# A hybrid encoder layer on one Trainium2 core: PSUM banks, gates, reciprocal roots and x blocks of the first pass

## The chip, the cores and the metric

The kernel runs on one core of a Trainium2 chip. Its engines are TensorE (PE), VectorE (DVE), ScalarE (ACT), GpSimd (POOL) and SyncE (SP, which here only issues DMAs); each runs its own list of instructions in order, and they wait for one another by semaphores. The metric is the device time of one execution in microseconds. Before the change it was 2523.88 us, the median of three runs (2520.88 to 2533.51).

## The reference

Two sequences of 2048 tokens (prompt and sample), 1024 features, go through one layer with the same weights.

```python
hx = rms_norm(x, pre_g)
proj = hx @ w_in                                   # 1024 -> 3088 columns
a_u, a_z, b_qkv, b_z, b_gates, c_qkv, c_z, d_q, d_z = split(proj)
y_a = fourier_mix(a_u, w_fnet) * silu(a_z)         # FFT over tokens and features
y_b = gdn_branch(b_qkv, b_gates, ...) * silu(b_z)  # 5-tap convolution, gated DeltaNet, both directions
y_c = neighbourhood_attn(c_q, c_k, c_v, rpb) * silu(c_z)
y_d = memory_attn(d_q, rms_norm(mem, mem_g), w_mem_kv) * silu(d_z)
out = x + rms_norm(concat(y_a, y_b, y_c, y_d) @ w_out, post_g)
```

Every `rms_norm` and `l2_norm` needs a reciprocal square root of a mean or a sum of squares.

## The kernel before, in words

Products are made in three matmuls of fp16 halves (high by high, high by low, low by high), so a weight is split once into `hi` and `lo` (`wnext`, L388 to L421) and x is split per block (`xblock`, L448).

The first pass (`pass_a`, L540) takes x in 16 blocks of 256 tokens, eight for each request (r = 0, 1). For a block, `xblock` loads two tiles of 128 tokens (`xt`), ScalarE sums the squares (L458), `rsqrt` (L232) makes the reciprocal root in eleven small VectorE operations (two on integers, then three rounds of three), ScalarE and VectorE write the halves `xh` (L466, L213), and two DMA transposes put them into `xT` (L468). From `xT` TensorE makes the units k, q, v (48 matmuls each, L484 to L486) and ag, which is 256 columns for the Fourier branch and 16 gate columns (2 times 24 matmuls, L494 to L496). Each unit has one of two PSUM banks with the tag `mm` in turn. ScalarE drains a bank to `st` (L561, L568) and stores it to DRAM (`braw`, `au`); the 16 gate columns are drained by VectorE (L569). A copy of `xT` goes to DRAM (`xTd`, L551) for the later passes.

The next stage, `gdn_pre` (L931), runs beside the first pass. For each of 16 tiles of 256 tokens `conv_pair` reads `braw` back with two tokens of either neighbour (`craw`, L885; two buffers) and convolves it: one ScalarE operation (L889) and four VectorE operations (L891) for each half of k, q and v. `norms` (L911) calls `rsqrt` on 16 columns for each tile. `gdn_gates` makes the decays. After that come the Fourier branch, the triangular solve (`gdn_sub`, VectorE and GpSimd), the memory attention, the recurrence over 32 steps (`gdn_chain`) with the neighbourhood attention beside it, and the output projection (`pass_o`). The second and third projections (`pass_b`, `pass_z`) fill TensorE beside them. `rsqrt` is called 18 times in `xblock` (two of them for the memory tokens), 16 times in `norms`, 8 times in `gdn_out` and 17 times in `pass_o`.

What stands where on an engine is not written by hand: the tile framework simulates the engines while it builds, and by its own costs and the priority of each `band` (L202) chooses the next instruction. So a change of one instruction can move many others. SP's DMAs run in the order in which they are listed, and a DMA that waits holds up those behind it.

At the start of the program SP also writes zeros around `braw` of both requests (L518, L519): columns of two floats, 768 rows each.

## Time and profile before

| | |
|---|---|
| median of three runs | 2523.88 us |
| profiled execution | 2518.5 us, its span 2516.7 us |
| PE, DVE busy | 2006.7 us (80%), 2013.1 us (80%) |
| ACT, POOL busy | 1034.4 us (41%), 1128.9 us (45%) |
| mean granted TensorE clock | 0.919 |

The profile is of one execution, and 1.8 us of its time lie outside its span. Stages are found by their tiles: the first convolution operation starts at 119.8 us, the first pass drains its last bank at 653.9 us, the last tile of `gdn_pre` ends its convolution at 857.9 us, the recurrence runs from 1472 to 2112 us, and the matmuls of the output projection from 2152 us. Busy shares are to be read stage by stage; the table of stretches further down gives them.

### The profile page before, as it was taken

What the parts mean: (1) busy time and instruction counts of PE and PEld (TensorE: products, weight loads), DVE (VectorE), ACT (ScalarE), POOL (GpSimd) and SP (SyncE); (2) the same over time, 40 slices, a digit from 0 to 9 for tenths busy, and PEclk for the clock granted to TensorE, in tenths of its full rate; (3) what the DMA queues carried; (4) which work ended last, traced back from release to release, by engine and by line L of the source; (5) the groups of instructions that cost most, each with busy time, mean ns of one, the idle gap of its engine ahead of it and who ended that gap; (6) DMA issues with size and microseconds to landing.
All of it is one profiled execution on the core that took longest, in us unless ns stands there. A gap on an engine that the chain in (4) does not pass through costs nothing. (4 is left out here: it accounts for less than half of the span.)

```text
span 2516.7 us, 60042 instructions
## 1 busy us (share of the span) xinstructions
PE 2006.7 (80%) x23715; PEld 1701.4 (68%) x23715; DVE 2013.1 (80%) x4757; ACT 1034.4 (41%) x2434; POOL 1128.9 (45%) x1181
## 2 busy tenths in 40 slices
PE   0787778787446786899698988887788899899998
PEld 0665667665335675777576767777677788688887
DVE  3579988989999979668989667887679977677774
ACT  1455554553354421334056423554445523332322
POOL 1225655445476667535786152232234343533220
PEclk9988899998768988999799999999999999899999
DMA  9899899999635694599789877999999995555543
GB/s 94 193 210 178 200 232 239 233 209 234 180 94 159 168 222 118 142 218 179 153 187 200 181 195 210 229 199 210 198 214 224 217 279 164 169 182 187 187 161 118
DMA packets 827484, 476.08 MB, mean 189 GB/s; under 512 B 556864, under 2 KB 789952, under 8 KB 818752
## 3 DMA queue, kind: packets, MB, share of 16 engines
q1 hardware_dynamic: 802624, 438.67, 76.0%
q10 hardware_dynamic: 24576, 33.56, 4.5%
q8 instruction: 186, 3.05, 0.5%
q14 instruction: 98, 0.80, 0.1%
HBM read 243.38 MB, written 163.73 MB: 162 GB/s over the span
## 5 line engine op out<-in xcount | busy, mean ns | idle before, releaser
L484 PE MATMUL pj<-xT,w 128*128 128x256 f16 x2592 | 741.1, 286 | 119.7 <-DMA xT<-xh 35.7
L486 PE MATMUL pj<-xT,w 128*128 128x256 f16 x2592 | 739.5, 285 | 4.0 <-POOL w L421 4.0
L485 PE MATMUL pj<-xT,w 128*128 128x256 f16 x2592 | 740.6, 286 | 0.0
L485 PEld LDWEIGHTS <-w 128*128 128x128 f16 x2592 | 265.1, 102 | 109.4 <-issue 67.7
L484 PEld LDWEIGHTS <-w 128*128 128x128 f16 x2592 | 265.1, 102 | 102.7 <-issue 31.4
L486 PEld LDWEIGHTS <-w 128*128 128x128 f16 x2592 | 265.3, 102 | 52.8 <-POOL w L421 9.4
L502 PE MATMUL po<-w,oy 128*128 128x256 f16 x1024 | 280.3, 274 | 1.4 <-DVE oy L716 1.4
L500 PE MATMUL po<-w,oy 128*128 128x256 f16 x1024 | 280.7, 274 | 0.8 <-ACT oy L715 0.8
L501 PE MATMUL po<-w,oy 128*128 128x256 f16 x1024 | 280.9, 274 | 0.0
L891 DVE SCALAR_TENSOR_TENSOR cacc<-craw,cws,cacc 128x256 f32<-128x256 f32 x384 | 244.4, 671 | 7.4 <-ACT cacc L889 6.2
L494 PE MATMUL pj<-w,xT 128*128 128x272 f16 (+1 forms) x512 | 153.3, 300 | 43.8 <-ACT st L561 21.8
L230 POOL TENSOR_TENSOR oy<-oy,oz 128x512 f32<-128x512 f32 x60 | 101.0, 1704 | 187.7 <-ACT oy L701 179.4
L1165 POOL COPY bk<-rA 64x512 f16<-64x512 f16 x124 | 85.8, 692 | 208.9 <-PE pw L502 171.2
L765 ACT ACTIVATE oj<-po,wsc_o 128x256 f32<-128x256 f32 x128 | 59.5, 469 | 243.9 <-PE po L502 243.1
L495 PE MATMUL pj<-w,xT 128*128 128x272 f16 (+1 forms) x512 | 153.0, 299 | 0.8 <-POOL w L421 0.8
L496 PE MATMUL pj<-w,xT 128*128 128x272 f16 (+1 forms) x512 | 152.9, 299 | 0.0
L421 POOL TENSOR_TENSOR w<-wt,w 128x512 f16<-128x512 f32 (+1 forms) x70 | 85.1, 1223 | 145.9 <-ACT w L419 118.4
L227 POOL TENSOR_TENSOR mP<-mP,mP 128x1024 f16<-128x1024 f32 x32 | 71.6, 2241 | 137.0 <-DVE ty L1503 52.9
L500 PE MATMUL pno<-nPT,nv 128*128 128x64 f16 x704 | 78.5, 199 | 57.9 <-DMA nPT<-np__2819_27983 20.2
L1170 DVE COPY b<-rA 64x1536 f16<-64x1536 f16 x128 | 112.4, 878 | 8.1 <-DMA cT<-T 3.7
L227 POOL TENSOR_TENSOR km<-kt,km 128x256 f16<-128x256 f32 x128 | 96.4, 775 | 38.0 <-ACT km L1009 36.2
L1485 ACT ACTIVATE mP<-pms,ty,mds 128x256 f32<-128x256 f32 x128 | 71.0, 560 | 97.7 <-DVE ty L1482 76.0
(442 smaller groups left out, 6162.7 us busy)
## 6 DMA issues: line engine op xcount, KB each, us to landing
xT<-xTd SPq DMA_DIRECT2D x32, 1024.0 KB
rec<-km SPq DMA_DIRECT2D x32, 768.0 KB
rA<-rec SPq DMA_DIRECT2D x64, 384.0 KB
xTd<-xT SPq DMA_DIRECT2D x16, 1024.0 KB
sz<-st ACTq DMA_DIRECT2D x64, 256.0 KB
oz<-sz SPq DMA_DIRECT2D x16, 1024.0 KB
out_dram<-oo SPq DMA_DIRECT2D x32, 512.0 KB
craw<-braw SPq DMA_DIRECT2D x48, 260.0 KB
```

Source lines behind the costliest of these rows:

```text
L227: self.nc.gpsimd.tensor_tensor(out=out, in0=a, in1=b, op=ALU.subtract)
L484: nc.tensor.matmul(ps, whi, xhi, start=(kt == 0), stop=False)
L485: nc.tensor.matmul(ps, whi, xlo, start=False, stop=False)
L486: nc.tensor.matmul(ps, wlo, xhi, start=False, stop=(kt == KT - 1))
L494: nc.tensor.matmul(ps, xhi, whi, start=(kt == 0), stop=False)
L495: nc.tensor.matmul(ps, xhi, wlo, start=False, stop=False)
L496: nc.tensor.matmul(ps, xlo, whi, start=False, stop=(kt == KT - 1))
L500: nc.tensor.matmul(ps, whi, xhi, start=start, stop=False)
L501: nc.tensor.matmul(ps, whi, xlo, start=False, stop=False)
L502: nc.tensor.matmul(ps, wlo, xhi, start=False, stop=stop)
L891: nc.vector.scalar_tensor_tensor(out=acc[:, f], in0=raw[:, f, t:t + CB], scalar=w[:, t:t + 1], in1=acc[:, f], op0=ALU.mult, op1=ALU.add)
L1170: nc.vector.tensor_copy(b1[s, :, h].rearrange("p (d x) c -> p d x c", d=2), ra[s, :, 0:12])
```

## The change

Five edits. `rsqrt` starts from one integer operation in place of two, and has one Newton round of three operations and one round of higher order of four: eight operations in place of eleven. The gate columns are drained by ScalarE in place of VectorE. In the first pass the units take four PSUM banks in turn: the two of `mm`, and those with the tags `s` and `t`, which attention and the Fourier branch use later. The first two x blocks of request 0 are transposed by TensorE (through the banks `s` and `t`, copied to `xT` by ScalarE) in place of the DMA. `craw` has four buffers, and the scheduler is told to list the load of `craw` behind the second unit after the next block's unit of the same name, and the first convolution operation behind the fourth (`behind`: an order for the scheduler, with no semaphore).

```diff
+    def behind(self, ins, i):
+        if i < len(self.gseq):
+            self.tc.add_manual_dep(ins.ins if hasattr(ins, "ins") else ins, self.gseq[i],
+                                   mybir.DependencyInfo(mybir.DependencyClass.NoSync, mybir.DependencyReason.DATA), reason="pace")
...
-        nc.vector.tensor_scalar(out=y.bitcast(I32), in0=x.bitcast(I32), scalar1=1, scalar2=None, op0=ALU.logical_shift_right)
-        nc.vector.tensor_scalar(out=y.bitcast(I32), in0=y.bitcast(I32), scalar1=-1.0, scalar2=float(0x5F3759DF),
-                                op0=ALU.mult, op1=ALU.add)
-        for i in range(3):
-            eng.scalar_tensor_tensor(out=t, in0=y, scalar=-0.5, in1=y, op0=ALU.mult, op1=ALU.mult)
-            eng.scalar_tensor_tensor(out=t, in0=t, scalar=1.0, in1=x, op0=ALU.mult, op1=ALU.mult)
-            eng.scalar_tensor_tensor(out=(out if i == 2 else y), in0=t, scalar=1.5, in1=y, op0=ALU.add, op1=ALU.mult)
+        stt = lambda o, a, s, b, op: eng.scalar_tensor_tensor(out=o, in0=a, scalar=s, in1=b, op0=op, op1=ALU.mult)
+        nc.vector.tensor_scalar(out=y.bitcast(I32), in0=x.bitcast(I32), scalar1=-0.5, scalar2=float(0x5F3759DF), op0=ALU.mult, op1=ALU.add)
+        stt(t, y, -0.5, y, ALU.mult)
+        stt(t, t, 1.0, x, ALU.mult)
+        stt(y, t, 1.5, y, ALU.add)
+
+        c = math.sqrt(0.375)
+        stt(t, y, c, y, ALU.mult)
+        stt(t, t, 1.0, x, ALU.mult)
+        stt(t, t, -1.25 / c, t, ALU.add)
+        stt(out, t, 1.875, y, ALU.add)
...
-            nc.sync.dma_start(dst[:, :, :, t * P:t * P + P].rearrange("p l k t -> p (l k) t"), hl.rearrange("p l c -> p (l c)"), transpose=True)
+            if pe:
+                for l in range(2):
+                    pt = self.pat.tile([P, KT, P], F16, name=self.nm("pxt"), tag=PSS[l])
+                    for k in range(KT):
+                        nc.tensor.transpose(pt[:, k], hl[:, l, k * P:k * P + P], self.ident16)
+                    nc.scalar.activation(dst[:, l, :, t * P:t * P + P], pt, AF.Copy)
+            else:
+                nc.sync.dma_start(dst[:, :, :, t * P:t * P + P].rearrange("p l k t -> p (l k) t"), hl.rearrange("p l c -> p (l c)"), transpose=True)
...
+    def bank(self, wide):
+        self.nbank += 1
+        if wide and self.nbank % 2:
+            return self.pat.tile([P, 2, 256], F32, name=self.nm("pj"), tag="st"[self.nbank // 2 % 2])
+        return self.pmm.tile([P, 2, 256], F32, name=self.nm("pj"), tag="mm")
...
-            xT = self.xblock(x[tb * 256:tb * 256 + 256, :])
+            xT = self.xblock(x[tb * 256:tb * 256 + 256, :], pe=r == 0 and tb < 2)
...
-                nc.vector.tensor_scalar(out=self.gates[r][:, 2 * tb + t, :], in0=ps[:, 256:272], scalar1=d, scalar2=None, op0=ALU.mult)
+                nc.scalar.activation(self.gates[r][:, 2 * tb + t, :], ps[:, 256:272], AF.Copy, scale=d)
...
-        raw = pp.tile([P, 2, CB + 4], F32, name=self.nm("craw"), tag="craw", bufs=2)
-        nc.sync.dma_start(raw, self.D[f"braw{r}"][:, 2 * i:2 * i + 2, tb * CB:tb * CB + CB + 4])
+        raw = pp.tile([P, 2, CB + 4], F32, name=self.nm("craw"), tag="craw", bufs=4)
+        g = self.gidx[r, min(tb + 1, 7), u]
+        self.behind(nc.sync.dma_start(raw, self.D[f"braw{r}"][:, 2 * i:2 * i + 2, tb * CB:tb * CB + CB + 4]), g + 2)
...
-            nc.scalar.activation(acc[:, f], raw[:, f, 0:CB], AF.Copy, scale=w[:, 0:1])
+            self.behind(nc.scalar.activation(acc[:, f], raw[:, f, 0:CB], AF.Copy, scale=w[:, 0:1]), g + 4)
```

Three places show how the order moves. The first is SP's list near its start (`w` with 128x8x64 rows are weights of v, `xt_654` and `xt_658` the two tiles of the second x block). Before:

```order
L456 DMA xt_654<-in_x_prompt_dram 128x1024
L518 DMA braw_3153<-ty_3154 768x1x2
L519 DMA braw_3153<-ty_3154 768x1x2
L468 DMA_TRANSPOSE xT_107<-xh_133 128x16x128
L468 DMA_TRANSPOSE xT_107<-xh_137 128x16x128
L385 DMA w_369<-in_w_in_dram 128x8x64
L385 DMA w_464<-in_w_in_dram 128x8x256
L385 DMA w_464<-in_w_in_dram 128x8x16
L551 DMA xTd_0_216<-xT_107 128x4096
L456 DMA xt_658<-in_x_prompt_dram 128x1024
```

And now, where `xt_689` and `xt_693` are those two tiles and `xt_1094` is the first of the third block:

```order
L469 DMA xt_689<-in_x_prompt_dram 128x1024
L548 DMA braw_3196<-ty_3197 768x1x2
L549 DMA braw_3196<-ty_3197 768x1x2
L469 DMA xt_693<-in_x_prompt_dram 128x1024
L469 DMA xt_1094<-in_x_prompt_dram 128x1024
L398 DMA w_404<-in_w_in_dram 128x8x64
L398 DMA w_499<-in_w_in_dram 128x8x256
L398 DMA w_499<-in_w_in_dram 128x8x16
L398 DMA w_2784<-in_w_in_dram 128x8x256
L581 DMA xTd_0_251<-xT_107 128x4096
```

The block's transposes are gone from the list, and the next x tiles have moved ahead of the weights of v and ag; the writes of zeros stay ahead of all of these.

The second is VectorE at the same time (`w_277` is q's raw weight, `w_369` v's; L415 scales, L431 takes the largest magnitude). Before:

```order
L409 TENSOR_SCALAR ty_279<-gpre,wsc_q 128x8
L333 TENSOR_REDUCE ty_628<-ty_623 32x1
L415 TENSOR_TENSOR wt_301<-w_277,ty_279 128x512
L415 TENSOR_TENSOR wt_305<-w_277,ty_279 128x512
L334 STREAM_TRANSPOSE pmb<-ty_628 32x32
L335 COPY ty_620<-pmb 32x1
L336 COPY ty_620<-pmb 32x1
L337 COPY ty_620<-ty_620 64x1
L431 TENSOR_REDUCE ty_377<-w_369 128x2 x4
L415 TENSOR_TENSOR wt_309<-w_277,ty_279 128x512
L415 TENSOR_TENSOR wt_313<-w_277,ty_279 128x512
```

And now (`w_312` is q's raw weight, `xh_710` and `xh_733` the second block's tiles; the largest magnitudes of v and of ag stand eleven and four rows above the first of these):

```order
L222 SCALAR_TENSOR_TENSOR xh_710<-xt_689,ty_698,xh_710 128x1024
L370 TENSOR_SCALAR wsc_q<-ty_331 128x1
L372 TENSOR_SCALAR wsc_q<-ty_331 128x1
L222 SCALAR_TENSOR_TENSOR xh_733<-xt_693,ty_698,xh_733 128x1024
L447 ISA ty_505,ty_510<-ty_505,agpre 128x8
L447 ISA ty_510 128x1
L367 TENSOR_SCALAR ty_424<-p2t_419 128x1
L422 TENSOR_SCALAR ty_314<-gpre,wsc_q 128x8
L369 TENSOR_SCALAR ty_426<-ty_424 128x1
L428 TENSOR_TENSOR wt_336<-w_312,ty_314 128x512
L428 TENSOR_TENSOR wt_340<-w_312,ty_314 128x512
```

The scaling of q's weight has moved behind the second x block and behind the raw weights of v and ag.

The third is SP's list around the first raw load (`craw`). Before:

```order
L456 DMA xt_1271<-in_x_prompt_dram 128x1024
L551 DMA xTd_1_217<-xT_652 128x4096
L885 DMA craw_12925<-braw_209 128x2x260
L468 DMA_TRANSPOSE xT_1022<-xh_1048 128x16x128
L468 DMA_TRANSPOSE xT_1022<-xh_1052 128x16x128
```

And now:

```order
L488 DMA_TRANSPOSE xT_1092<-xh_1115 128x16x128
L581 DMA xTd_1_252<-xT_687 128x4096
L488 DMA_TRANSPOSE xT_1092<-xh_1119 128x16x128
L469 DMA xt_1342<-in_x_prompt_dram 128x1024
L469 DMA xt_1698<-in_x_prompt_dram 128x1024
L581 DMA xTd_2_253<-xT_1092 128x4096
L919 DMA craw_12947<-braw_244 128x2x260
L469 DMA xt_1702<-in_x_prompt_dram 128x1024
```

The first raw load has moved from ahead of the third block's transposes to behind them and behind the store of that block.

## Rows read from the trace of the kernel before

**Rows 1.** Busy time and share of each engine, from the page.
```profile
PE 2006.7 (80%) x23715; PEld 1701.4 (68%) x23715; DVE 2013.1 (80%) x4757; ACT 1034.4 (41%) x2434; POOL 1128.9 (45%) x1181
```
**Rows 2.** Stretches by stage: bounds, length, busy us (instructions) of each engine.
```profile
core 0: us, PE busy (x) PEld busy (x) DVE busy (x) ACT busy (x) POOL busy (x), PEclk, DMA share, GB/s
0.00:120.00 120.00, 47.53 (x348) 36.72 (x349) 51.17 (x202) 35.10 (x61) 21.99 (x26) 0.96 0.97 140
120.00:200.00 80.00, 59.29 (x510) 48.00 (x510) 64.91 (x196) 43.47 (x93) 30.18 (x28) 0.88 0.97 206
200.00:858.00 658.00, 464.99 (x4232) 382.76 (x4232) 621.39 (x1512) 308.71 (x686) 376.02 (x395) 0.84 0.84 193
858.00:1472.00 614.00, 514.94 (x5270) 418.73 (x5268) 502.29 (x937) 229.01 (x531) 366.45 (x391) 0.92 0.82 179
1472.00:2112.00 640.00, 534.95 (x9908) 475.75 (x9909) 502.08 (x1348) 291.53 (x733) 217.47 (x266) 0.96 0.93 215
...
2152.00:2516.00 364.00, 352.03 (x3162) 311.02 (x3162) 241.16 (x464) 106.96 (x297) 100.42 (x60) 0.98 0.47 165
```
**Rows 3.** Waits of VectorE from 0 to 200 us: sum, times, longest.
```profile
DVE ty L431 <- DMA w<-in_w_in_dram: 41.6, 4, 21.3
DVE ty L431 <- DMA w<-in_w_mem_kv_dram: 11.7, 2, 6.4
```
**Rows 4.** Waits of VectorE from 200 to 858 us, the longest.
```profile
DVE xh L213 <- ACT xh L466: 10.1, 7, 4.6
```
**Rows 5.** Lines L244 and L569, 120 to 858 us: ns min/median/max, starts.
```profile
L244 DVE SCALAR_TENSOR_TENSOR ty<-ty,ty x45: 140/161/1186, 131.6 to 559.7; 128x2 f32<-128x2 f32 x45
L244 DVE SCALAR_TENSOR_TENSOR ty<-ty,nrm x45: 156/174/1148, 176.6 to 846.6; 128x16 f32<-128x16 f32 x45
...
L569 DVE TENSOR_SCALAR gates<-pj,wsc_ag x30: 187/227/235, 135.2 to 660.0; 128x16 f32<-128x16 f32 x30
```
**Rows 6.** Groups of L244, 120 to 858 us: busy us, mean ns, idle before.
```profile
L244 DVE SCALAR_TENSOR_TENSOR ty<-ty,nrm 128x16 f32<-128x16 f32 x45 | 18.2, 404 | 0.4
L244 DVE SCALAR_TENSOR_TENSOR ty<-ty,ty 128x2 f32<-128x2 f32 x45 | 15.3, 339 | 0.7
```
**Rows 7.** Waits of TensorE from 60 to 654 us, the longest.
```profile
PE pj L484 <- DMA xT<-xh: 35.7, 4, 23.3
PE pj L484 <- DVE gates L569: 33.4, 11, 6.5
PE pj L494 <- ACT st L561: 21.8, 10, 6.1
```
**Rows 8.** SP's queue in order of time, 36 to 66 us: start, duration.
```profile
37.13 0.52 SPq L518 DMA_DIRECT2D braw<-ty  x1
...
38.44 23.85 SPq L468 DMA_TRANSPOSE xT<-xh  x2
62.38 2.18 SPq L385 DMA_DIRECT2D w<-in_w_in_dram  x3
```
**Rows 9.** ScalarE in order of time, 96 to 122 us: start, duration, idle before.
```profile
97.42 0.39 ACT L568 ACTIVATE st<-pj 128x256 f32<-128x256 f32 x1 [0.20 <-PE pj L496]
109.93 0.58 ACT L561 ACTIVATE st<-pj 128x512 f32<-128x512 f32 x1
...
119.27 0.91 ACT L889 ACTIVATE cacc<-craw,cws 128x256 f32<-128x256 f32 x2 [2.75 <-DMA craw<-braw]
120.60 0.58 ACT L561 ACTIVATE st<-pj 128x512 f32<-128x512 f32 x1
```
**Rows 10.** Groups over the whole span: busy us, mean ns, idle before.
```profile
L421 POOL TENSOR_TENSOR w<-wt,w 128x512 f16<-128x512 f32 x66 | 80.3, 1224 | 143.9 <-ACT w L419 116.4 <-DVE ty L333 22.0 <-DMA w<-in_w_out_dram 5.3
...
L466 ACT ACTIVATE xh<-xt,ty 128x1024 f16<-128x1024 f32 x36 | 39.4, 1144 | 43.1 <-DVE ty L463 43.1
...
L502 PE MATMUL p<-kq,kbd 128*128 128x128 f16 x128 | 28.4, 240 | 0.0
```

27 lines of the change are left out of this document (18 added, 9 removed).

## The prediction

> **What bounds the kernel now.** I read the busy times of the whole span first, then the stretches by stage, then the waits of the two busy engines in the early stretches, and last SP and ScalarE in order of time at the start. Over the span PE and DVE are equally busy, 80% each [rows 1], which says nothing of a bound. The stretches do [rows 2]. From 0 to 120 us neither works much: DVE is busy for 51 us and PE for 48. From 200 to 858 us, where the first projections and the convolution tiles run, DVE is busy for 621.4 of 658 us (94%), and PE for 465.0 (71%). From 858 to 1472 us DVE has 82% and PE 84%, in the recurrence 78% and 84%, and in the output projection PE has 352 of 364 us. So VectorE bounds the stretch up to 858 us, mixed chains the middle, and TensorE the end. The pace says the same: the gates of the first pass end at 660.0 us while the `rsqrt` of `norms` runs from 176.6 to 846.6 us [rows 5], so 15 blocks take (660.0 - 97.4)/15 = 37.5 us each [rows 5, 9] and 15 tiles (846.6 - 176.6)/15 = 44.7 us each. The convolution falls behind the projections, so what counts there is VectorE's time per tile, and TensorE's waits count only where they starve it.
>
> **The change part by part.** The sum is made against the profiled execution (2518.5 us, 1.8 of it outside the span), which is 5.4 us below the median of the runs and 2.4 below the lowest.
>
> *Roots and gates.* Each `rsqrt` loses three small VectorE operations. After 120 us and before 858 us lie 45/3 = 15 calls on two columns and 15 on sixteen [rows 5], and 30 of the 32 gate drains of 0.227 us (6.8 us). What is one small operation worth? Its median is 0.161 us on two columns and 0.174 on sixteen, its longest 1.19 [rows 5], and its mean 0.339 and 0.404 [rows 6]. By medians 90 operations give 15 x 3 x 0.161 + 15 x 3 x 0.174 = 15.1 us, with the gates 21.9; by means 15.3 + 18.2 = 33.5, with the gates 40.3. The rest of the mean is not work: an operation on two columns that takes 1.19 us has been held up, and GpSimd is busy for 376 of the 658 us [rows 2]. If the holder is a GpSimd operation, the next VectorE operation inherits the wait when this one is gone, so I stay near the medians and take 25 us, with 21.9 and 40.3 as ends.
>
> The Trainium skill says it as a rule that speaks against counting the means (SBUF — State Buffer, "Who interferes with whom"): a VectorE instruction with two SBUF inputs contends with a GpSimd instruction that reads SBUF, and whichever starts second is blocked for the whole of the other. By that rule the removed operations are worth their own time alone, and this term is 21.9 us; by the mean of the rows it is 40.3. The gap of median and mean agrees with the rule; that the wait passes on is shown by no row.
>
> On ScalarE the 32 gate drains cost at most 32 x 0.39 = 12.5 us (by the drain of 256 columns [rows 9], the nearest above) and at least nothing. ScalarE is busy for 309 of 658 us there [rows 2], so idle time takes them; were ScalarE the bound, they would cost those 12.5 us.
>
> *The start.* Of the first 200 us VectorE is idle for 68.8 + 15.1 = 83.9 [rows 2]. 41.6 + 11.7 = 53.3 of these wait for raw weights [rows 3], and the change does not bring weights sooner. The zeros around `braw` go out at 37.13 us, the transposes issued behind them take 23.85 us to issue, and the last quarter of v's weight follows at 62.38 [rows 8]. Now the transposes are gone from the list, but the next x tiles, v and ag still stand behind the zeros, so they land near 62 to 70 us as before. TensorE can transpose block 0 and make its k while it would have waited (23.3 us is its longest wait for `xT` [rows 7]): 64 transposes of at most 0.240 us and 8 copies of at most 1.144 [rows 10] are 15.4 us of PE and 9.2 of ACT, half of them before 64 us in idle time, the other half beside the weights' splitting. But VectorE's list now scales q's weight behind the second x block and behind v and ag. So q, v and ag all split after the raw ag weight has landed, 12 operations in a row on GpSimd of 1.224 us [rows 10] = 14.7 us, where before q's four (4.9 us) were done ahead of it. Block 0 then ends where it did, at 97.4 us [rows 9], or up to 4.9 later: the early product of k buys nothing by itself.
>
> What it buys is the second block. Its second x tile stood behind the transposes and now is ahead of the weights, so its `xT` is ready when block 0 ends. Before, its k was drained at 109.93 and its q only at 120.60, since ScalarE stood at the first convolution until the raw load had come at 119.27 [rows 9], and a bank was not free. Now no convolution stands there and four banks are in turn, so I expect blocks 1 and 2 to run without such gaps, some 15 us sooner. The convolution gains less, for its first operation is listed behind the fourth unit after. It starts about when it did (119.8 us), with more x blocks prepared. For the 200 us I take a gain of 10. The ends are 83.9 - 53.3 = 30.6 (all idle time but that for weights) and a loss of 15, where the first convolution starts one unit trio (some 25 us) later and 10 us of other work fills that time.
>
> *From 200 to 858 us.* VectorE's idle time is 658 - 621.4 = 36.6 us; the largest single cause is the x block's high half, 10.1 us [rows 4]. TensorE waits 33.4 us for gate drains and 21.8 for ScalarE's drains up to 654 us [rows 7]. Those go with the gates on ScalarE and four banks; what is late next is VectorE itself, so they do not count as time. I take 8 us for an earlier x and four raw buffers; the ends are 36.6 and a loss of 10.1, the same wait once more.
>
> *After 858 us.* The same work is left. The recurrence loses 8 x 3 operations in `gdn_out`, 4.2 us by the median of sixteen columns and 9.7 by the mean; VectorE is busy for 78% there, and I take 3. In the output projection the roots lie under matmuls but for the last, 3 x 0.16 = 0.5 us. That the list is made anew can shift this part either way. VectorE is idle for 111.7 us from 858 to 1472 and for 137.9 in the recurrence [rows 2]; I allow a twelfth of their sum, 20 us, to either side and take zero.
>
> **Sum:** 25 + 10 + 8 + 3 + 0.5 = 46.5, so 2518.5 - 46.5 = 2472. The median may stand up to 5.4 above such a profile as it does before; I say **2474 us**. The bounds of the first three terms and of the order together would give from 2391 to 2542, but they do not come all at once; the likeliest case has 2445 to 2503 for itself.
>
> **Rivals.** *A, VectorE's idle time goes too.* If the early blocks follow each other closely and the raw loads are there in time, the stretch up to 858 us is filled: 27 for operations, 30 at the start, 20 of 36.6, and 5 later are 82, so 2436 us. For it: TensorE's waits of 55 us go at a stroke, and SP's list has x far ahead. Against it: 53.3 us of the early waits are for weights, and waits between 200 and 858 are scattered over many causes, no larger than 10.1.
>
> *B, the gain is given back later.* From 858 us neither engine is above 84%, and the recurrence is a chain of 32 steps with the attention and the projections beside it. If the new order there is worse by some 30 us of the 250 that VectorE idles, or if projections not yet made at 858 us lengthen the recurrence, the sum shrinks to 5 to 15: 2510 to 2518 us, no change. For it: the list is made anew by costs that are not the chip's. Against it: the units made before each stage are nearly the same in number, so no work is put off.
>
> *C, the raw loads come too late.* Now each tile's load stands behind the second unit after its neighbour's, and SP issues in order. If VectorE starves once per tile, 16 tiles at 4.3 us (somewhat over the 2.75 us that ScalarE waited for the first load [rows 9]) cost 69 us, so with the 46.5 gained the result is 2518.5 + 22 = 2541 us. It decides from 46.5/16 = 2.9 us a tile. For it: the load also stands behind the store of a block's `xT`, which waits for its transposes. Against it: blocks come every 37.5 us and tiles are eaten every 44.7, so after some tiles the load has time, and four buffers hold it.
>
> **How the numbers follow.** The forecast has 0.62, A 0.18, B 0.12, C 0.08. A measurement of this kernel can tell about 0.5% from no change: faster is below 2511, slower above 2536. Faster takes the forecast, A and a quarter of B: 0.83. Same takes the rest of B and a little of C: 0.10. Slower is 0.07. The range from 2425 to 2516 holds the forecast, most of A and half of B; it leaves out some 0.04 of A, 0.06 of B and C, 0.18 together.
>
> **What would show it.** In the profile of the changed kernel the drains of block 0 should still end near 97 us and q of the second block should be drained within 10 us of its k; the first convolution should start between 115 and 130 us; VectorE's busy time up to its last `norms` should be 25 to 40 us less, with the end of that stage near 815 us in place of 858, and the recurrence should start that much sooner and last as long as before. TensorE should wait no more for gates. The prediction is wrong if the stage ends before 800 us (A), if it ends near 815 and the recurrence or what is ahead of it takes 30 us longer (B), or if VectorE waits for raw loads in most tiles (C). If means and not medians give the worth of a small operation, VectorE's busy time falls by 40 us or more.

## The result and the profile after

The changed kernel took 2546.93 us (median of 5, 2541.26 to 2549.59) where the kernel before took 2523.88 (5, 2520.88 to 2533.66): a ratio of 1.0076, with a 95% interval of 1.0050 to 1.0102. It is slower; I had said 2474 us and faster. A second comparison (e18 below) gave 1.0133 (1.0108 to 1.0157). The two intervals do not meet, so a ratio moves by some 0.3% beyond its interval from one comparison to another, and differences of that size are marked as small below.

First the changed kernel's busy line from its page (profiled execution 2545.39 us, span 2543.6), then its stretches. Their bounds are its own: the first convolution of VectorE, the last, the first product of the recurrence and its last, and the output projection.

```profile
PE 2021.8 (79%) x23779; PEld 1713.4 (67%) x23779; DVE 1985.6 (78%) x4548; ACT 1043.2 (41%) x2474; POOL 1134.0 (45%) x1181
```
```profile
0.00:156.00 156.00, 78.41 (x576) 61.15 (x577) 61.89 (x221) 56.82 (x97) 26.34 (x30) 0.78 0.79 140
156.00:868.00 712.00, 504.32 (x4586) 416.11 (x4584) 660.25 (x1562) 342.06 (x783) 402.86 (x419) 0.84 0.84 192
868.00:1501.00 633.00, 520.29 (x5240) 418.15 (x5240) 531.30 (x943) 230.98 (x547) 375.60 (x393) 0.89 0.79 174
1501.00:2142.00 641.00, 537.05 (x9959) 480.79 (x9957) 493.31 (x1314) 287.02 (x717) 210.61 (x264) 0.96 0.92 216
2180.00:2543.00 363.00, 351.11 (x3162) 310.64 (x3162) 210.53 (x414) 106.99 (x297) 102.31 (x60) 0.98 0.46 165
```

VectorE did lose work: 2013.1 us [rows 1] became 1985.6, 27.5 less. But against [rows 2] the first convolution starts at 155.7 us and not 119.8 (36 later); the convolution stage is 26 us shorter (712.5 for 738.1); the stretch from there to the recurrence is 18.5 longer (633.3 for 614.8), though it holds nearly the same work; the recurrence and the end are the same to 3 us. The sum is the 26.9 us by which the span grew. A second pair of profiles, taken together on one chip, gives the same first three terms (e17 and e18): +37.5, -21.9, +18.8. Its recurrence is 14.2 us shorter in the changed kernel, so that those two spans differ by 16.9 us only; e17's profiled execution is the longest of its ten (2545.81 us for a median of 2536.44).

The shorter stage is not all a gain. 10.6 us of VectorE's work now stand ahead of the first convolution (61.6 us busy there for 51.0). Up to the last convolution VectorE is busy for 722 us where it was 737, so 15 us of work are gone (6 in the second pair), and its idle time there has grown by 25 us (22 in the second pair), all of it ahead of the first convolution: in the stage itself it is 51.7 us in both. After the last convolution, VectorE's busy time up to the recurrence is 29 us longer (531.3 for 502.3) for nearly as many instructions.

Where the start went is in four views. VectorE's waits of the changed kernel from 0 to 200 us, the longest (to be read against [rows 3]):

```profile
DVE ty L473 <- ACT xq L471: 50.1, 5, 26.5
DVE ty L444 <- DMA w<-in_w_in_dram: 20.4, 2, 16.2
DVE xh L222 <- ACT xh L479: 20.2, 4, 16.6
```

SP's queue from 42 us (against [rows 8]), and further down, to the first raw load:

```profile
42.55 27.00 SPq L398 DMA_DIRECT2D w<-in_w_in_dram  x2
69.65 2.37 SPq L581 DMA_DIRECT2D xTd<-xT  x1
...
136.32 0.38 SPq L919 DMA_DIRECT2D craw<-braw  x1
```

And ScalarE in order of time (against [rows 9]): block 0's last drain, k and q of the second block, the first convolution step, each with start and duration:

```profile
112.97 0.27 ACT L602 ACTIVATE gates<-pj,wsc_ag 128x16 f32<-128x16 f32 x1
...
127.60 0.60 ACT L592 ACTIVATE st<-pj 128x512 f32<-128x512 f32 x1 [7.28 <-PE pj L506]
...
134.84 0.58 ACT L592 ACTIVATE st<-pj 128x512 f32<-128x512 f32 x1
...
149.74 0.91 ACT L923 ACTIVATE cacc<-craw,cws 128x256 f32<-128x256 f32 x2 [0.25 <-ACT gates L602]
```

The longest wait is new: for 26.5 us VectorE stands at the second block's norm, whose x tile has not landed, and behind it in its list stand the operations that scale q's weight. Block 0's last drain comes at 113 us in place of 97. SP stands at 42.55 for 27.00 us although no transpose is there: the 23.85 us of [rows 8] were the queue's, not the transposes', so their going freed nothing. The second block's later x tile shows the same, by its issue on SP and its square on ScalarE. The changed kernel, then the kernel before:

```profile
38.96 1.95 SPq L469 DMA_DIRECT2D xt<-in_x_prompt_dram  x2
67.44 1.06 ACT L471 ACTIVATE xq<-xt 128x1024 f32<-128x1024 f32 x1 [17.39 <-DMA xt<-in_x_prompt_dram]
```
```profile
65.77 1.26 SPq L456 DMA_DIRECT2D xt<-in_x_prompt_dram  x2
73.59 1.06 ACT L458 ACTIVATE xq<-xt 128x1024 f32<-128x1024 f32 x1 [1.40 <-DMA xt<-in_x_prompt_dram]
```

It was issued 27 us sooner and used 6 us sooner. What filled the queue, no run here tests; the writes of zeros were issued just ahead, at 37.64 and 38.21 us, and stayed in every run. Then the first raw load, ordered behind a later projection, is issued at 136.32 (114.81 before), and ScalarE comes to its convolution step at 149.74 only, behind the next block's squares, for whose x it waits.

Between the last convolution and the recurrence one place can be shown. VectorE and GpSimd of the changed kernel at 1469 us (start, duration):

```profile
1469.62 16.03 DVE L1538 TENSOR_SCALAR ty<-ty,mds 128x4 f32<-128x4 f32 x1
1471.64 14.01 DVE L697 SCALAR_TENSOR_TENSOR st<-st,pj 128x512 f32<-128x512 f32 x1
```
```profile
1469.58 2.13 POOL L236 TENSOR_TENSOR mP<-mP,mP 128x1024 f16<-128x1024 f32 x1 [4.15 <-DVE ty L1537]
1471.64 7.85 POOL L812 MEMSET b<- 128x3072 f16 x3
1479.44 0.95 POOL L812 MEMSET bk<- 128x1024 f16 x1
1480.33 1.80 POOL L812 MEMSET b<- 128x2048 f16 x1
1482.08 3.55 POOL L812 MEMSET bw<- 128x2048 f16 x2
```

A scaling of 128x4 lasts until the last of eight GpSimd operations without a gap between them, 16.03 us, and VectorE's next instructions stand behind it. No edit touches these lines; they were apart in the order before. The stretch that holds it, from the end of the preparation to the recurrence, is 5 us longer (140.4 for 135.2). The other 13 lie before it, between the attention's first scores and the end of the preparation (262.4 for 249.1, and 260.5 for 247.0 in the second pair); what ends last there is not shown.

### The profile page after: what moved, and what is told of

The parts are those of the page before. It is cut to its first block, busy times and chain, and to the rows that moved or that the text cites. A ratio compares the mean times of both kernels' runs of the same rounds, so it can differ in the third digit from the quotient of the medians.

```text
span 2543.6 us, 59972 instructions
## 1 busy us (share of the span) xinstructions
PE 2021.8 (79%) x23779; PEld 1713.4 (67%) x23779; DVE 1985.6 (78%) x4548; ACT 1043.2 (41%) x2474; POOL 1134.0 (45%) x1181
## 5 line engine op out<-in xcount | busy, mean ns | idle before, releaser
L506 PEld LDWEIGHTS <-w 128*128 128x128 f16 x2592 | 264.1, 102 | 67.7 <-DVE w L434 15.1
L925 DVE SCALAR_TENSOR_TENSOR cacc<-craw,cws,cacc 128x256 f32<-128x256 f32 x384 | 233.4, 644 | 5.9 <-ACT cacc L923 5.3
L434 POOL TENSOR_TENSOR w<-wt,w 128x512 f16<-128x512 f32 (+1 forms) x70 | 90.9, 1305 | 68.7 <-ACT w L432 68.2
```

What stands on the lines that cost most here:

```text
L506: last = nc.tensor.matmul(ps, wlo, xhi, start=False, stop=(kt == KT - 1))
L925: nc.vector.scalar_tensor_tensor(out=acc[:, f], in0=raw[:, f, t:t + CB], scalar=w[:, t:t + 1], in1=acc[:, f], op0=ALU.mult, op1=ALU.add)
```

## The experiments

What each run showed, in one table: the ratio to the kernel before on its chip, then from its trace the start of the first convolution, the length of the convolution stage, of the stretch from there to the recurrence, and of the recurrence, in us.

| run | ratio (95%) | first conv. | conv. stage | to recurrence | recurrence |
|---|---|---|---|---|---|
| before | 1 | 119.8 | 738.1 | 614.8 | 639.2 |
| changed | 1.0076 (1.0050-1.0102) | 155.7 | 712.5 | 633.3 | 640.5 |
| e1 | 0.9982 (0.9965-0.9999) | 138.9 | 721.9 | 622.8 | 640.6 |
| e2 | 1.0022 (1.0006-1.0037) | 142.3 | 734.7 | 614.7 | 667.8 |
| e3 | 1.0019 (0.9998-1.0039) | 124.2 | 725.3 | 611.0 | 675.9 |
| e4 | 1.0136 (1.0114-1.0159) | 159.9 | 714.2 | 618.1 | 655.1 |
| e5 | 0.9907 (0.9882-0.9933) | 126.4 | 712.9 | 619.6 | 652.4 |
| e6 | 0.9813 (0.9792-0.9835) | 124.7 | 736.8 | 615.7 | 691.4 |
| e7 | 0.9992 (0.9972-1.0011) | 134.4 | 736.0 | 619.3 | 675.3 |
| e8 | 1.0115 (1.0097-1.0133) | 147.5 | 729.3 | 635.6 | 645.7 |
| e9 | 1.0060 (1.0042-1.0078) | 162.3 | 717.3 | 614.0 | 651.7 |
| e10 | 1.0008 (0.9990-1.0026) | 151.2 | 711.4 | 624.4 | 634.2 |
| e11 | 1.0193 (1.0169-1.0217) | 129.0 | 746.9 | 627.9 | 671.0 |
| e12 | 1.0029 (1.0012-1.0046) | 129.1 | 740.3 | 619.0 | 644.6 |
| e13 | 0.9966 (0.9942-0.9990) | 123.2 | 726.5 | 612.2 | 648.6 |
| e14 | 0.9902 (0.9880-0.9924) | 122.3 | 705.9 | 617.1 | 650.9 |
| e15 | 1.0055 (1.0036-1.0074) | 157.4 | 707.6 | 628.1 | 636.6 |
| e16 | 1.0169 (1.0145-1.0194) | 120.7 | 740.3 | 622.2 | 672.2 |
| e17 | 1.0005 (0.9989-1.0021) | 129.2 | 741.1 | 610.7 | 657.9 |
| e18 | 1.0133 (1.0108-1.0157) | 166.7 | 719.2 | 629.5 | 643.7 |

Before, e12 and e17 have the same order up to 860 us, and e6 up to 1470: their first convolution starts at 119.8, 129.1, 129.2 and 124.7. So 10 us in that column are nothing, and 19 us in the last, where before and e17 are the same program. Runs that share a chip can be compared most closely: e1 to e4 and e13 to e16 ran on one, e5 to e8 on a second, e9 to e12 on a third, e17 and e18 on a fourth.

**e1, without the transposes on TensorE.**

```diff
-            xT = self.xblock(x[tb * 256:tb * 256 + 256, :], pe=r == 0 and tb < 2)
+            xT = self.xblock(x[tb * 256:tb * 256 + 256, :], pe=False)
```


> The changed kernel with the first two x blocks transposed by DMA again, the other four edits kept. Theory S (the start): the changed kernel lost 36 us before its first convolution (155.7 us against 119.8 in the profiles) and 26 of them came back by the last convolution; the loss was made by the transposes on TensorE, which let the second block's VectorE work go ahead of the weights of q, v and ag of the first block (their scaling began at 80.1 us instead of 68.1) and put ScalarE copies between the drains. Then without them the first convolution starts at 138 to 144 us, the last one ends near 855, and the time is 2530 to 2535. Rival P (the pins): the raw loads and first convolution steps ordered behind later projections make the late start; then the first convolution stays at 150 us or later and the time at 2540 to 2548. Rival R (another order each time): what an edit does to the start counts for little beside the new order that it gives to all engines; then the stretch from the last convolution to the first step of the recurrence (614.8 us before, 633.3 in the changed kernel) is what moves, by 10 us or more, and the time can be anything from 2510 to 2550.

First convolution at 138.9 us, as theory S said; the time is better than it said (2527.48 us, and 2529.61 for the kernel before). The last convolution ends at 860.8, and the stretch to the recurrence is 8 us longer than before. P falls as the only cause.

**e2, without the raw loads' order.**

```diff
-        self.behind(nc.sync.dma_start(raw, ...), g + 2)
+        nc.sync.dma_start(raw, ...)
-            self.behind(nc.scalar.activation(acc[:, f], raw[:, f, 0:CB], ...), g + 4)
+            nc.scalar.activation(acc[:, f], raw[:, f, 0:CB], ...)
```
(and `craw` with two buffers)

> The changed kernel without its fifth edit: two raw buffers again and no ordering of raw loads and first convolution steps behind later projections; transposes on TensorE, gates on ScalarE, four banks and the shorter root are kept. Theory S: the transposes make the late start; the first convolution then starts at 145 to 152 us and the time is 2538 to 2545. Rival P (the pins): in the changed kernel the first raw load was issued 136.3 us into the span and the convolution step of ScalarE 149.7, behind two norms that waited for x; without the order the step stands right behind the load, the first convolution starts at 128 to 140 us, and the time is 2520 to 2532. Rival R: the stretch from the last convolution to the first step of the recurrence moves by 10 us or more beside that.

142.3 us, between the two expectations, so the pins too made the start late. But this order has a recurrence of 667.8 us (639.2 and 657.9 in the two profiles of the kernel before), which takes the gain: R's sign in another place.

**e3, the shorter root alone** (on the kernel before, the edit's first part and nothing else).

> The kernel before with the shorter reciprocal root alone (8 operations for 11). By the forecast's own sum its removed work is some 22 of the 25 us taken from VectorE, of which about 18 lie in the convolution stage: with the start as before (first convolution at 118 to 122 us) the last convolution ends near 836 to 842 and the time is 2500 to 2508, if the order after that is as good as before. Rival R: the new order gives it back between 858 and 1472 us or in the recurrence: 2515 to 2530 with the convolution stage shortened all the same. Rival I: the removed operations only leave VectorE idle longer, since it waits for raw loads and ScalarE: the stage keeps its 738 us and the time stays at 2521 to 2527.

R, and further than it said. The trace is 12 us ahead at the first product of the recurrence (1460.5 for 1472.7 us), and then the recurrence takes 675.9: the time is not better at all.

**e4, the fills on VectorE.**

```diff
-        self.b1 = self.bds(pool, "b1", [P, 24, 2, 64], F16, 3)
+        self.b1 = self.bds(pool, "b1", [P, 24, 2, 64], F16, 3, self.nc.vector)
```
(the same for `bk`, `b2` and `bw`)

> The changed kernel with the seven zero fills of the recurrence's block buffers given to VectorE instead of GpSimd; the orders are the same up to 1470 us. In the changed kernel a 128x4 scaling of VectorE at 1469.62 us took 16.03 us, beside a split and seven fills of GpSimd that ran without a gap from 1469.58 to 1485.63, and three instructions behind it waited too. Theory F (the fills hold the scaling): it then takes 0.2 to 2.2 us, the recurrence starts 5 to 13 us sooner (1488 to 1497 us instead of 1501.5), and the time is 2533 to 2541. Rival N: the recurrence's start is set by its loads and the T blocks (last pz at 1461 us), so it starts at 1499 to 1503 us as before and the time stays at 2543 to 2549.

F was right of the place: no scaling there takes over 2.11 us, and the recurrence starts at 1492.2 in place of 1501.5. It was wrong of the time: the order from 1470 us on is another, the recurrence takes 15 us longer, and the kernel is no faster than the changed one (1.0136, for 1.0076 and 1.0133). A local gain of 9 us is less than what a new order of the rest moves.

**e5, two of four taps left out.**

```diff
-            for t in range(1, 5):
+            for t in range(1, 3):
```


> The kernel before with two of the four VectorE taps of every convolution left out (the output is that of a shorter filter): 192 operations of 671 ns, 129 us of VectorE's work, all between 120 and 858 us. Theory D (the forecast's: what VectorE saves in the convolution stage arrives at the end): the stage shortens by 95 to 125 us and the time by 90 to 125, to 2400 to 2435. Theory W (the work moves): with the root alone 13 us were saved in the convolution stage and the recurrence became 36.7 us longer, with 121 projection products more in it; the stage shortens, but the projections that stood in it go into the later stages, which get longer by more than half of the saving: the stage shorter by 50 us or more, the recurrence and what stands around it longer, and the time 2470 to 2520. Rival I: the stage is not set by VectorE at all and keeps 700 us or more.

129 us of operations bring 24 us (0.93% of 2542.59). The stage shortens by 25, so the step of theory D fails in the stage itself and not after it; W said half the saving is lost later, and that is not so either. VectorE is busy for 595 of 713 us here, 84%, so it no longer sets the pace alone; what does, this run does not show.

**e6, z without its third product.**

```diff
+                if not two:
-                nc.tensor.matmul(ps, wlo, xhi, start=False, stop=(kt == KT - 1))
+                    nc.tensor.matmul(ps, wlo, xhi, start=False, stop=(kt == KT - 1))
```


> The kernel before with the third product left out of all z projections (their low weight halves are not used): 1024 of 9312 projection products, at the final stage's rate of one product in 0.115 us some 118 us of TensorE. Theory W (TensorE's projections fill every stage, and what doesn't go into one goes into the next): the time falls by 60 to 118 us, to 2400 to 2465, and the projections in the recurrence fall by 300 or more of 2203. Rival C (the recurrence goes at the pace of its own chain of VectorE, ScalarE and loads, and the projections beside it cost nothing): the recurrence stays at 630 us or more and the time falls by less than 30 us.

46 us less (2496.98, and 2542.59 before) of 118 us of products, below W's range and above C's. The final stage could begin at 2099 us, 69 before the recurrence ends. So TensorE's projections count for about 0.4 of their time, and neither engine bounds the middle alone.

**e7, root, gates and banks together** (the changed kernel without the edits that e1 and e2 take out).

> The first three edits together (root, gates on ScalarE, four banks) without the transposes on TensorE and without the raw loads' order. By the forecast's terms for these three, 25 us off VectorE and 8 of idle time: 2485 to 2500 if they arrive at the end. Theory W: the convolution stage is shorter by 15 to 30 us and the stages after it are longer by nearly as much: 2512 to 2530. Rival R (order): a start or a later stage that is 15 us longer for reasons of its own, 2530 to 2550.

No change, as W said, but not by its mechanism: the convolution stage is not shorter by more than 5 us. Its first convolution starts at 134.4 us, 10 later than e6's on the same chip, though neither the transposes nor the pins are in it.

**e8, the transposes alone** (on the kernel before).

> The kernel before with only the transposes of the first two x blocks moved to TensorE. Without this edit the changed kernel came to 0.9982 of the kernel before, with it to 1.0076: theory S says that the edit itself costs 15 to 28 us: 2543 to 2557 here, with the first convolution at 130 to 145 us instead of 119.8. Rival P (it costs only together with the order of the raw loads): first convolution at 117 to 128 us and 2520 to 2535.

Slower by 1.15%, 29 us. The first convolution is some 23 us later than in e6 on that chip, 7 come back in the stage, and the stretch after it is 20 us longer. S has the size nearly right, but more of it lies behind the last convolution than before it.

**e9, q first in VectorE's order.** The changed kernel with two more pins behind the last scaling of q's weight (`qsl`); they order and do not synchronise.

```diff
+            mx = nc.vector.tensor_reduce(mk[:, k:k + step], raw[:, k:k + step], ...)
+            if name in ("v", "ag"):
+                self.tc.add_manual_dep(mx.ins, self.qsl, ...)
...
+        if pe and hasattr(self, "qsl"):
+            self.tc.add_manual_dep(nrm.ins, self.qsl, ...)
```


> The changed kernel (all five edits), in which the maxima of the v and ag weights and the second block's norm stand behind the scaling of the q weights in VectorE's order; nothing is computed differently. In the changed kernel's trace q's maxima were read at 37 us, but the reduction that turns them into q's scale stood behind the second block's norm, which waited 26.5 us for x, and behind v's maxima, so that q was scaled from 80.1 us on, against 42.5 in the kernel before, and the first block's last drain came at 113 us against 97. Theory Q (this order is what the transposes on TensorE cost): q scaled from 42 to 50 us, block 0's last drain at 95 to 103 us, the first convolution at 138 to 147 us, and a ratio to the kernel before of 0.997 to 1.003 (1.0076 with all five edits). Rival S (the wait for v's load and for the raw loads sets the start): first convolution at 150 us or later and a ratio of 1.005 to 1.010. Rival R (a new order of the rest): the first convolution is sooner, but the stretch from the last convolution to the first product of the final stage (1312 us in the changed kernel, 1294 before) is 1315 us or more, and the ratio stays at 1.004 or above.

My theory Q falls. VectorE's waits in the first 167 us, the longest:

```profile
DVE wt L428 <- POOL w L436: 28.0, 1, 28.0
DVE ty L446 <- DMA w<-in_w_in_dram: 24.2, 2, 19.7
```

The wait of 26.5 us for x is gone and one of 28.0 for GpSimd has taken its place: q's third piece waits for a buffer that GpSimd frees late. ScalarE and GpSimd show why:

```profile
74.13 1.06 ACT L475 ACTIVATE xq<-xt 128x1024 f32<-128x1024 f32 x1 [20.05 <-DMA xt<-in_x_prompt_dram]
77.56 1.15 ACT L434 ACTIVATE w<-wt 128x512 f16<-128x512 f32 x2 [0.47 <-ACT st L598]
78.27 2.27 POOL L436 TENSOR_TENSOR w<-wt,w 128x512 f16<-128x512 f32 x2 [56.16 <-ACT w L434]
```

GpSimd's step waits for ScalarE's, and that one stands in ScalarE's list behind the square of the second block's x, for which ScalarE waits 20.05 us. So the wait for x was not removed; it moved from VectorE's list to ScalarE's. Block 0 ended at 116 us and the first convolution started at 162.3. S has the numbers right (a start at 150 us or later, a ratio of 1.0060), but the load that q stands behind is x's and not v's.

**e10, transposes on TensorE for block 0 alone.**

```diff
-            xT = self.xblock(x[tb * 256:tb * 256 + 256, :], pe=r == 0 and tb < 2)
+            xT = self.xblock(x[tb * 256:tb * 256 + 256, :], pe=r == 0 and tb < 1)
```


> The changed kernel with the transposes on TensorE for the first x block alone; the second goes by DMA as before. Theory Q: the second block's norm still stands ahead of q's scaling in VectorE's order (its rows 97 and 100 against 106), so q is scaled no sooner than 75 us, the first convolution starts at 143 to 157 us and the ratio is 1.004 to 1.010. Rival S2 (the second block's transposes on TensorE, behind the whole first block's projections, make the late start): q's scaling is late as well, but the first convolution starts at 130 to 142 us and the ratio is 0.998 to 1.003.

The start is as Q said (151.2 us, 22 later than e12's on the same chip; q is scaled from 87.0 us, and VectorE's longest wait is again for the second block's x, 30.1 us), the ratio as S2 said. A start that is 22 us later and a kernel that is not slower: the two must not be read as one.

**e11 and e12, new orders for the same work.**

```diff
         e = pp.tile([P, 2, CB], F32, name=self.nm("cexp"), tag="cexp", bufs=2)
+        if r == 0 and tb == 0:
+            nc.vector.memset(e[:, 0, 0:1], 0.0)
```
```diff
             nc.gpsimd.memset(zero, 0.0)
+            nc.gpsimd.memset(zero, 0.0)
```


> The kernel before with three fills of a 128x1 column added in the first convolution tile (values that are written over later; under 1 us of work). It moves 2242 of VectorE's 4271 rows and 931 of ScalarE's 1787, from about 150 us on. Theory R (the order before is a good draw, and any edit redraws it): of eight other orders run so far the stretch from the last convolution to the final stage's first product took 1285 to 1328 us, 1315 on average, against 1294 before; so 5 to 35 us longer in all, a ratio of 1.002 to 1.014. Rival N (a new order alone moves the time by less than the measurement tells): a ratio of 0.997 to 1.002.

> The kernel before with one fill of a 128x64 tile of zeros (0.15 us on GpSimd) done twice in the blocks of the recurrence's preparation. The order is the same up to the middle of that stage and moves 1005 of VectorE's rows after it. Theory R: the time changes by 5 to 30 us, a ratio of 1.002 to 1.012, all of it after 1080 us. Rival N: 0.998 to 1.002.

R in e11: three fills of a column cost 49 us (0.0193 of 2536.38), more than the whole change. In e12 one fill done twice cost 7 us, R's by the interval but no more than the 0.3% by which comparisons differ. The stretches of e11:

```profile
129.00:876.00 747.00, 523.73 (x4688) 429.22 (x4688) 684.96 (x1714) 352.17 (x785) 401.28 (x426) 0.83 0.86 193
876.00:1504.00 628.00, 517.79 (x5281) 419.01 (x5279) 529.86 (x941) 227.43 (x532) 371.51 (x391) 0.92 0.80 175
1504.00:2175.00 671.00, 552.23 (x9910) 495.73 (x9909) 499.58 (x1339) 290.74 (x725) 214.34 (x263) 0.92 0.90 204
```

VectorE's busy time of the second row is 27.6 us above that of [rows 2] for nearly the same work, 502.29: its instructions got longer, as in the changed kernel (531.30), and the scaling at 1471 us again takes 16.0.

**e13 and e14, the order kept and the work changed.** After the build has ordered the instructions, e13 takes out three operations of each root (and moves what they signal to the operation ahead of each); e14 cuts two taps of the convolution to one column. Of e14's edit:

```diff
+    for k, ins in enumerate(bb.instructions):
+        if ins.name in SHORT:
+            bb.instructions[k] = copy.replace(ins, ins=[cut(p) for p in ins.ins], outs=[cut(p) for p in ins.outs])
```


> The kernel before with the shorter root, in the order before: the 177 operations that the new formula doesn't need (3 in each of 59 calls) are taken out after the order was made, and all 4110 other operations of VectorE, and every instruction of the other engines, stand as in the kernel before. Theory R (the order cost what the edits gained): with the order kept the time falls, by the forecast's 18 to 22 us for this edit if what is saved arrives at the end: a ratio of 0.990 to 0.994. Theory W (the time saved on VectorE hardly arrives: 24 of 129 us arrived with two taps left out): 2 to 6 us, a ratio of 0.997 to 1.000. With the root alone and a new order the ratio was 1.0019.

> The kernel before, in the order before, with two of the four VectorE taps of every convolution cut to one column after the order was made (the output is that of a shorter filter but for those columns): 192 operations of 671 ns become 192 of 60 to 250 ns, so 80 to 117 us are taken off VectorE between 120 and 858 us. With the two taps left out and a new order the time fell by a ratio of 0.9907 only. Theory R (the new order ate the rest): the convolution stage shortens by 60 us or more and the ratio is 0.960 to 0.978. Theory W (other limits stand close behind VectorE in this stage: x loads, raw loads, ScalarE's steps): the stage shortens by 15 to 40 us and the ratio is 0.984 to 0.994.

e14 is W's by all its numbers; e13 lies between the two, next to W. The stretches of e13, then of e14, each from the first convolution to the recurrence (beside 741.00 and 611.00 us in e17):

```profile
123.00:850.00 727.00, 524.60 (x4748) 431.96 (x4748) 671.79 (x1618) 353.08 (x779) 410.90 (x423) 0.83 0.88 198
850.00:1462.00 612.00, 512.33 (x5265) 415.80 (x5264) 502.76 (x936) 228.48 (x531) 373.17 (x392) 0.92 0.82 180
```
```profile
122.00:828.00 706.00, 516.93 (x4746) 427.91 (x4745) 632.92 (x1707) 351.51 (x778) 396.71 (x423) 0.85 0.90 203
828.00:1445.00 617.00, 510.51 (x5271) 416.71 (x5269) 503.62 (x939) 228.75 (x531) 367.30 (x391) 0.92 0.81 179
```

The root with the order kept is 9 us faster than the kernel before (2517.67 and 2526.66, 0.1 to 0.6%), where with a new order on the same chip (e3) it was not faster (1.0019, from 0.9998); the two intervals do not meet. In the stage, the lines of the roots lost 28 to 32 us (83.0 us for 115.3 before and 110.6 in e17), but VectorE's busy time only 8 to 15 (671.8 for 686.4 and 680.0): most of the waits that left with the removed operations came back in others. In e14 the taps' lines show why so little came of 192 cut operations. The groups of the taps in the kernel before, then in e14 (busy us, mean ns, idle before):

```profile
L891 DVE SCALAR_TENSOR_TENSOR cacc<-craw,cws,cacc 128x256 f32<-128x256 f32 x384 | 244.4, 671 | 7.4 <-ACT cacc L889 6.2
```
```profile
L891 DVE SCALAR_TENSOR_TENSOR cacc<-craw,cws,cacc 128x256 f32<-128x256 f32 x192 | 132.5, 718 | 7.6 <-ACT cacc L889 7.2
L891 DVE SCALAR_TENSOR_TENSOR cacc<-craw,cws,cacc 128x1 f32<-128x1 f32 x192 | 62.5, 350 | 0.6
```

An operation on one column takes 350 ns on average. That mean has two parts: 139 of the 192 take 111 to 221 ns, and the 53 others 279 to 1297, each of which ends 11 to 20 ns after a GpSimd operation did. One such pair:

```profile
208.93 1.12 DVE L891 SCALAR_TENSOR_TENSOR cacc<-craw,cws,cacc 128x1 f32<-128x1 f32 x1
```
```profile
208.85 1.19 POOL L421 TENSOR_TENSOR w<-wt,w 128x512 f16<-128x512 f32 x1 [1.39 <-ACT w L419]
```

The taps left whole hardly changed: the 671 is the mean of all four taps, and at the places of these 192 the kernel before took 707 ns for the 718 here. So a held operation stays held until GpSimd is done, however short it is itself. Of 129 us, 49.4 left the engine (80 to 117 were expected), the stage became 32 to 35 us shorter, and 25 arrived.

**e15 and e16, new orders around both kernels** (the fill of e11, in the second convolution tile).

```diff
+        if r == 0 and tb == 1:
+            nc.vector.memset(e[:, 0, 0:1], 0.0)
```


> The changed kernel with three fills of a 128x1 column added in the second convolution tile (written over later; under 1 us of work). They move 2139 of VectorE's 4040 rows, from some 230 us on, and nothing else. Theory R: the changed kernel's own time is one draw of many, and another lies anywhere from 2500 to 2590 us, a ratio to the kernel before of 0.990 to 1.025, with 8 us or more between it and the 1.0076 of the changed kernel. Rival N (the 0.76% belongs to the five edits): 1.005 to 1.010.

> The kernel before with the same three fills in the second convolution tile instead of the first: 2227 of VectorE's rows move. The first draw of this kind came to 1.0193. Theory R: again slower, 1.003 to 1.020, since the order before is a good one and a redraw forgets it. Rival L (the first draw was one bad place, as a VectorE operation held by GpSimd's fills): 0.997 to 1.003.

e16 is R again, 1.0169. e15 lies 0.2% under the changed kernel's first ratio and 0.8% under its second: R's kind of result by the second, N's by the first, so it does not decide. Its start (157.4 us) lies ahead of the first moved row, so it is the changed kernel's late start once more and no new draw of it.

**e17 and e18, both kernels once more.**

> The kernel before, unchanged: a second profile. If single profiles can be compared stage by stage, the first convolution starts within 10 us of 119.8 us, the convolution stage takes 735 to 742 us, the stretch to the recurrence 612 to 618 and the recurrence 636 to 645. If the recurrence takes 646 us or more, the 9 and 12 us that it was longer with the order kept are no loss of these kernels, and what they saved before it arrives at the end in full. The ratio is 0.998 to 1.002.

> The changed kernel, unchanged: a second profile and a second ratio on the same chip as the kernel before. If the first account stands, the first convolution starts 25 to 40 us later than in the other kernel's profile of this chip, the convolution stage is 20 to 30 us shorter, the stretch to the recurrence 10 to 20 us longer, and the ratio lies between 1.005 and 1.011; the 128x4 scaling beside GpSimd's fills near 1470 us again takes more than 10 us.

The start, the stage and the stretch after it repeat (e17's stretch of 610.7 us is just under my 612). e18's ratio is above what I expected, and the scaling near 1490 us took 7.29 us, under my 10. The recurrence of e17 is 657.9 us, so single profiles cannot be compared there, and the 9 and 12 us in e13 and e14 need be no loss of theirs.

## Why the prediction was wrong, point by point

**The terms against the result.** The sum was 46.5 us gained, and 26.9 were lost. VectorE's work up to the last convolution fell by 15 us (forecast 25). Its idle time ahead of the first convolution grew by 25 (forecast 10 less). Its idle time in the stage stayed as it was (forecast 8 less). The stretch after the stage grew by 18.5 (forecast 0). The recurrence and the end together lost 1.9 (forecast 3.5). Without the 18.5 the kernel would still have been 8 us slower in this pair, so the start alone turned the sign, and the new order made the loss three times as large.

**The roots and gates (25 us): too much, by 10 us or more.** The sign that I had named, 25 to 40 us less of VectorE's busy time up to its last `norms`, came out as 15 (737 to 722), and as 6 in the second pair. The 27.5 us of the whole span agree with my 25 by luck: VectorE has some 30 us less to do in the output projection, and loses some 29 again between the stage and the recurrence. The kept order says what the roots are worth in time: 9 us of the whole run (2 to 15), 12 to 15 of the stage. I had 15.1 for them in that stage by medians and 33.5 by means, and the median was the right reading of the time, though the mean was the right one of what the roots' own lines would lose (28 to 32). The sentence that no row showed, that a wait passes on to other operations, is shown by e13: VectorE as a whole lost 8 to 15 us there.

The Trainium skill's rule that I weighed (SBUF — State Buffer, "Who interferes with whom": the one that starts second is blocked for the whole of the other instruction) agrees with e14's 53 held operations, which end 11 to 20 ns after a GpSimd operation. The same section of the Trainium skill says that a scaling (tensor_scalar) can enter a mode that contends with GpSimd for the shared port pair; the 16.03 us agree with a lock of that kind, but go past the rule, since the block lasted over eight instructions and not one.

**The start (+10, with a loss of 15 as the end): the step that failed first.** The first convolution came 36 and 37.5 us later in two pairs of profiles. I had seen that q's weight would be scaled behind the second block, and concluded that block 0 ends "where it did, or up to 4.9 later"; it ended 15.6 us later, because I priced GpSimd's splitting and not VectorE's standing for 26.5 us at the second block's norm. e9 says that another order on VectorE alone would not have mended it, since ScalarE then stands at the same x. I had read SP's 23.85 us as the transposes' cost [rows 8] and expected the second x tile early, since it no longer stood behind them; they were the queue's, and the tile came 6 us sooner. And I took the convolution's place behind the fourth later unit as costing one trio at worst, while it stood behind whole norms that wait for x. The transposes make the start late by themselves (e8, 23 us later than e6 on its chip), and the pins add 15 to 18 us on top of them (142.3 in e2, 159.9 and 157.4 in e4 and e15, on one chip). That the pins do so alone is not shown: e1 has them without the transposes and starts at 138.9, but e7, which has neither, at 134.4. What the transposes cost in the whole run is not settled either: taking them out gave back 0.9% (e1) and putting them in alone cost 1.15% (e8), but fills that compute nothing moved as much. The second block did run q within 7.2 us of k, as I said; nothing came of it.

**200 to 858 us (8 us): not seen.** The stage became 26 and 22 us shorter where I had 33 with the roots and gates, but 10.6 and 11.5 of that stand ahead of its start now, and VectorE's idle time in it is the same (51.7 us twice; 61.1 and 57.3 in the second pair). TensorE's waits for gates went, from 33.4 us [rows 7] to one of 3.1 and one of 1.1 for the gates on ScalarE, and they did not count as time, as I said.

**The new order (zero, 20 us to either side): the second step that failed.** After the stage the changed kernel had made up all but 10 us (868.2 for 857.9). The 18.5 us after it go with no one edit: e9 has all five and takes 614.0 us there, e2 has the transposes among its four and takes 614.7, and e8 has the transposes alone and takes 635.6. Three builds with a few tiny fills and no other change were slower by 0.3, 1.7 and 1.9%. The stretch from the last convolution to the recurrence took 610.7 and 614.8 us in the kernel before and 611.0 to 635.6 in all others. In the twenty profiles that stretch goes with VectorE's busy time in it, for nearly the same instructions: 502 to 505 us where it takes 611 to 619 (six profiles), 522 to 532 where it takes 622 to 636 (six). So what an order costs there is seen at least in part as time inside VectorE's instructions; no run tested this by itself. The order of the kernel before is a good draw among the few that were tried, and a new one is not centred on zero: I should have taken a loss and not 0. How large, these runs are too few to say, and the one new order of the changed kernel (e15) was not slower. With the order kept the same root is faster.

**Rivals.** B named the right place ("the list is made anew by costs that are not the chip's") and got 0.12; its second half, projections put off into the recurrence, is only seen in part, 2284 products there for 2203. C's starving in each tile did not come: VectorE's wait at the convolution is 5.9 us in the whole run, and ScalarE's waits for raw loads, 16.8 us before, are gone from its list. A fell with the start.

What stays open: whether any of the 18.5 us can be laid to one of the five edits (I think none), why five of the orders have a recurrence of 668 to 676 us and the others (e6 aside) 634 to 658, and why two comparisons of the same pair differ by 0.6%.

## What to carry to other kernels

Where a build orders the instructions of all engines anew, time any edit against a build that is ordered anew for no reason, and if the order at hand is a good one, look for a way to keep it: the smaller root was worth 9 us in the old order and nothing in the new one that was timed. Count a removed small operation by its median, and not all of that, while another engine holds what it waits for (15.1 us by medians, 8 to 15 off VectorE in e13). Where a stage is told by its first and last operation, count the engine's busy time from the start of the program too: a stage can get shorter because work moved ahead of it. And when a wait is moved out of one engine's list, look whose list it stands in next. A queue that stands at an instruction says when the queue got free, not what that instruction costs.

## What I had not expected of the hardware

- A VectorE scaling of 128x4 took 16.03 us beside eight GpSimd operations without a gap (7.29 us in another execution, 16.0 in e11). Operations on one column take 111 to 221 ns, or until 11 to 20 ns after the GpSimd operation that holds them (279 to 1297 ns).
- The same program differs more between two profiles in some stages than in others: the convolution stage 738.1 and 741.1 us, the recurrence 639.2 and 657.9.
- Early work on TensorE with a pause behind it gave the next products no higher clock. The changed kernel, then the kernel before, from 60 to 80 us:

```profile
60.00:80.00 20.00, 1.64 (x6) 1.15 (x6) 10.64 (x41) 4.97 (x7) 0.18 (x1) 0.50 0.72 205
```
```profile
60.00:80.00 20.00, 14.76 (x113) 11.67 (x114) 11.49 (x38) 5.88 (x10) 4.58 (x4) 1.00 1.03 277
```

The granted clock is 0.50 after k's early product and a pause of 28.5 us, the lower of its two levels. The 1.00 of the kernel before is not what its first products had: its profile holds no reading of the clock ahead of 68.1 us, and a product's time tells the level. The kernel before, where it changes, then the changed kernel:

```profile
67.72 0.42 PE L485 MATMUL pj<-xT,w 128*128 128x256 f16 x1
68.11 0.27 PE L484 MATMUL pj<-xT,w 128*128 128x256 f16 x1
```
```profile
93.96 0.42 PE L505 MATMUL pj<-xT,w 128*128 128x256 f16 x1
94.53 0.27 PE L505 MATMUL pj<-xT,w 128*128 128x256 f16 x1
```

The products took 0.42 us from 64.4 to 68 us before, where they ran without a gap, and from 81.5 to 94 us in the changed kernel, where TensorE was busy for 5.2 us of the ten from 80 to 90.
